# Moving gate transfers to GpSimd's queue and adding 11 places for raw weights in the feed-forward phases of a two-block transformer kernel

## The chip, the cores and the metric
The kernel runs on one core of a Trainium2 chip. The metric is the device time of one execution in microseconds (us). TensorE (PE) multiplies matrices, VectorE (DVE) and ScalarE (ACT) work elementwise, GpSimd (POOL) does almost nothing here, and SyncE (SP) only issues DMA transfers. Each engine takes its own instructions in a fixed order, and an instruction that waits holds up all that stand behind it on the same engine. This goes for the issuing of transfers as well.

## The reference
256 tokens of width 1024 in float32 pass through two blocks.

The first block has a mixer (latent attention with rotary positions, and a pooling branch), an attention over a memory of 256 rows, a mixture of 32 experts (two chosen for each token), and a norm.

The second block has two layers. What matters here is one layer, cut to this:

```python
mod = silu(c) @ ada_w[l] + ada_b[l]                 # 9 vectors of 1024
sh1, sc1, g1, sh2, sc2, g2, sh3, sc3, g3 = split(mod, 9)
n1 = rms_norm(h, norm_g[l, 0]) * (1 + sc1) + sh1
h = h + 0.5 * g1 * swiglu(n1, wg[l, 0], wu[l, 0], wd[l, 0])
n2 = rms_norm(h, norm_g[l, 1]) * (1 + sc2) + sh2
h = h + g2 * token_mixing(n2, ...)                  # two attentions, gates, an output product
n3 = rms_norm(h, norm_g[l, 2]) * (1 + sc3) + sh3
h = h + 0.5 * g3 * swiglu(n3, wg[l, 1], wu[l, 1], wd[l, 1])
```

`swiglu(x, wg, wu, wd)` is `(silu(x @ wg) * (x @ wu)) @ wd` with an inner width of 2816. So there are four feed-forward phases, and six gate vectors g that scale columns of a result.

## The kernel before, in words
**Weights come as a stream.** Every weight is used once, in pieces of 128 partitions by 1024 float32 columns (512 KB). A recording pass of the kernel notes the order of use; then the class `Stream` puts out, in that order, the load of a piece (on SP's queue, `w`), and for a piece of kind S its split into two parts of lower precision whose sum is the weight: `whi`, a rounded copy made by ACT in two halves (L205), and `wlo`, the rest `w - whi`, made by DVE in two halves (L212). PE needs three products for each pair of operands (L432 to L434: `whi` by the activations' high part, `wlo` by the high part, `whi` by the low part).

**Places.** A raw piece takes one of `N_RAW` = 4 places from its load until its `wlo` is made; `whi` and `wlo` have 8 places each (`N_HI`), held until PE has used the piece. `pump` issues what has a place: splits run up to 8 pieces ahead of PE, and loads at most 4 pieces ahead of the splits. A load therefore waits, on SP, for the DVE instruction that frees the place it will overwrite.

**Modulation pieces.** Pieces of kind A hold rows of the transposed `ada_w`. DVE multiplies each with silu(c) and sums along the row (`ajunk`, L623, two instructions of 512 columns and two short reads of the accumulator); eight pieces make one vector, a column tile `acolt`. `plan` lays 144 such pieces between the others: 16 early ones, and then 36, 16, 28, 28, 12 and 8 in the six phases of the second block (feed-forward, mixing, feed-forward, for each layer). They use raw places too.

**Gates.** A finished gate vector (`ada_finish`, L636 and L637) has to lie along the rows: its 1024 values are written from the column tile to DRAM (`gate`), and read back broadcast to all partitions (`growt`). Both transfers are issued by SP, so they stand between loads of weights, and the second waits for the first to land. The result is read by `res_gate` (L1509, tile `rg`) at the end of the phase that the gate belongs to.

**A feed-forward phase** (`ffn`) runs over 11 blocks of 256 inner columns. For block i, PE makes the two products of the gate and up weights (4 pieces, tile `ps`, 12 matmuls for each piece and both tiles of 128 tokens), ACT applies silu (`si`, L1543) and DVE multiplies (`pr`, L1545). While that happens PE does the down products of block i-1 (2 pieces, accumulated in `facc`), and between those of the first and the second tile of tokens it transposes `pr` (L438, `ps<-cst,pr`), which ACT and DVE split again (`hTh`, `hTl`). So PE waits for `pr`, and `pr` stands on DVE behind the splits and sums of pieces that are needed some 7 pieces later.

Every phase has a memory pool of its own, laid over the memory of the phase before; a tile of the new phase waits only for the last users of the tiles that lay there.

Of the kernel before, what the change touches and what calls it, by code (L numbers as in the profile page):

```python
# [18 lines left out]
P = 128  # L19
# [17 lines left out]
N_RAW = 4  # L37
N_HI = 8
# [7 lines left out]
# ---------------------------------------------------------------------------  # L46
# constants that depend on shapes alone
# ---------------------------------------------------------------------------
def _constants():
# [4 lines left out]
    # moe: [t', t] = 1 where t' < t  # L54
# [7 lines left out]
    # block 1 attention: chunk mask rows, added as two more rows of the contraction  # L62
# [6 lines left out]
    c["maskrows"] = np.stack([mq, mk], axis=1)  # [2, (q,k), S]  # L69
# [9 lines left out]
    )  # [p, g, t', tok]  # L79
# [3 lines left out]
    # block 2: axial angles, distances  # L83
# [4 lines left out]
    cs = np.stack([np.cos(ang), np.sin(ang)], axis=1).astype(np.float32)  # [S, 2, sec, 16]  # L88
# [8 lines left out]
# ---------------------------------------------------------------------------  # L97
# layout of the inputs
# ---------------------------------------------------------------------------
# [48 lines left out]
class Piece:  # L148
# [7 lines left out]
    def half(self, i):  # L156
        """Columns 512 i to 512 i + 511 of a piece of kind R."""
        if self.tag is None and len(self.place[0]) == 2:
            return self.place[0][i]
        raw = self.place[0][0] if self.tag is None else self.raw  # L160
        return raw[:, i * 512:(i + 1) * 512]


class Stream:
    """The weights in the order of their use: loads run ahead as far as slots are free. Kind S is split
    into two float32r parts ahead of its use; R is used as it is; A goes into a
    modulation vector."""

    def __init__(self, K, order):
        self.K = K  # L170
        self.rec = order is None
        self.order = [] if order is None else order
        self.pos = self.i_dma = self.i_hi = self.i_lo = self.clock = 0
        self.live = {"raw": 0, "hi": 0, "lo": 0}
        self.cap = {"raw": N_RAW, "hi": N_HI, "lo": N_HI}
        self.hold = math.inf  # from this piece on, no splits yet but those that must
        self.extra = []  # more places for pieces of kind R: its tiles, whether it can be used again
        self.deferred = []
        self.ada_done = {}

    def _load(self, p, tag):
# [7 lines left out]
        else:  # L189
            self.live[tag] += 1  # L190
            p.raw = K.wpool.tile([P, PIECE], F32, name="w", tag=tag, bufs=self.cap[tag])
            K.nc.sync.dma_start(p.raw[:, : p.n], K.piece_ap(p))

    @staticmethod
    def _halves(p):
        """In two, so that short steps of other chains get in between sooner."""
        return [slice(c, min(c + 512, p.n)) for c in range(0, p.n, 512)]
# [18 lines left out]
    def pump(self, upto=-1, raw=N_RAW):  # L216
        """Puts out the steps that can run by now, and those of the pieces up to a position anyhow."""
# [4 lines left out]
        while moved:  # L222
# [28 lines left out]
            while self.i_dma < len(order):  # L251
                p = order[self.i_dma]
                tags = ["raw", "hi", "lo"] if p.kind == "R" and self.i_lo >= self.i_dma else ["raw"]
                tag = next((x for x in tags if live[x] < cap[x]), None)
# [5 lines left out]

    def hold_after(self, n):
        """Holds back the splits after those of the next n pieces of kind S."""
# [46 lines left out]
    # modulation vectors: a piece for each 128 rows  # L309
# [28 lines left out]
def plan(order):  # L338
    """Places the pieces of the modulation weights among the others."""
# [11 lines left out]
    at = []  # (position, piece)  # L351
# [7 lines left out]
    # of the others, so many in each phase of the second block: the vector engine has more else to do in some  # L359
# [27 lines left out]
class Kernel:  # L387
# [28 lines left out]
    def load(self, dst, src):  # L416
        """Behind what is traced so far on its queue's engine, so not ahead of weights that are due before."""
# [22 lines left out]
    def rsqrt(self, y, v, t, scale, n=1):  # L440
        """y = scale * v ** -0.5 (all [P, n]; t is scratch): a first guess (within 3.4%) from the bits; then
        y <- ((v y^2)^2 + c1 v y^2 + c0) y, the minimax step within that range, which takes b v^-0.5 to
        (b^5 / k) v^-0.5 within 2.6e-5; then Newton's y <- (v y^2 - 3 g^2) y, from g v^-0.5 to -2 g^3 v^-0.5."""
# [20 lines left out]
    def warm(self, n, after=None, tag="mm"):  # L464
        """Products whose results nobody reads, so that the array's clock is not gated down while it has to wait."""
# [14 lines left out]
    def ss(self, dst, src, scale=1.0):  # L480
        """dst [P, 1] = sum of the squares of scale * src (up to 512 columns)."""
# [6 lines left out]
    def rstd(self, st, width, two=True):  # L488
        """(sum of squares / width + eps) ** -0.5 from the sums in st[:, 0:2]."""
# [8 lines left out]
    def split_T(self, hi, lo, src, gain=None):  # L498
        """hi/lo float32r of src * gain, gain per partition."""
# [8 lines left out]
    def transpose_split(self, hi, lo, src, kts, t, k0=0):  # L508
        """hi/lo[:, k0 + k, t's tokens] = src[:, k's columns] ^ T."""
# [29 lines left out]
    def dense(self, name, hi, lo, kt, width, src, evac, cb=512, tag="acc", outer=None, mid=None, pre=None, post=None):  # L539
        """A generator: for each block of columns, out[t] = x[t] @ w, then evac(t, b, out). Groups of  # L540
        outer blocks take all of one tile of tokens before the other; else the tiles take turns at each
        piece. mid follows the first group's first tile; pre(t, b) each evac; post(0)
        precedes the last tile's evac. Yields True between groups."""
# [66 lines left out]
    def c_silu(self):  # L610
        """silu(c) along the rows."""
# [3 lines left out]
    def ada_piece(self, l, m, i, raw):  # L615
        """128 outputs of a vector, by columns, from the transposed weights."""
# [9 lines left out]
    def ada_finish(self, l, m):  # L626
# [5 lines left out]
        elif m % 3 == 2:  # L632
            # along the rows, by way of DRAM
            d = self.dram.tile([D], F32, name="gate", tag="gate", bufs=2)
            col, r = r, self.ct([P, D], name="growt", tag="grow", bufs=3)
            nc.sync.dma_start(d.rearrange("(k p) -> p k", p=P), col)  # L636
            nc.sync.dma_start(r, d.unsqueeze(0).to_broadcast([P, D]))  # L637
        self.S.ada_done[(l, m)] = r

# [4 lines left out]
    def gain_row_pe(self, name, tile):  # L644
        """The same without a transfer for each partition; tile() gives places of 512 columns."""
# [15 lines left out]
    # =======================================================================  # L661
# [34 lines left out]
    def mixer(self, nrm):  # L696
# [3 lines left out]
        with self.phase("mix1") as pool:  # L700
# [14 lines left out]
            cs = self.ct([P, 2, 2, 16], name="cs")  # [p, (cos, sin), t, 16]  # L715
            rs = nrm.rs

            def tables():
                """rope tables of the positions"""
# [58 lines left out]
            def rope(x, t, heads, o1, o2):  # L778
                """x: [P, heads, 32] view, in place."""
# [39 lines left out]
            # pooling: d^T = u^T band, y^T = w^T d^T  # L819
# [9 lines left out]
            # gates and the pooling branch run between the steps of the attention  # L829
# [83 lines left out]
            def values(hp, p0, p1):  # L913
# [13 lines left out]
                # transposed, the two heads in their halves of the columns of the array  # L927
# [43 lines left out]
    def cross(self, nrm, pool):  # L971
# [26 lines left out]
        def to_T(dst, src, t, b):  # L998
            """dst[:, 4b.., t] = src ^ T, src [P, 512]."""
# [74 lines left out]
        # what the experts' phase starts with  # L1074
# [16 lines left out]
        # the output product, one tile of tokens after the other; the first two heads' half runs early  # L1091
# [56 lines left out]
    def moe(self, nrm, pool):  # L1148
# [16 lines left out]
        # the weights also use memory that other things need before or later  # L1165
# [1018 lines left out]
```

## Time and profile before

| | us |
|---|---|
| median of 3 runs | 1723.43 (1722.06 to 1725.42) |
| span of the profiled execution, first to last instruction | 1710.4 |
| median less that span | 13.0 |
| PE busy in the span | 1600.0 (94%) |
| DVE busy | 1139.6 (67%) |
| ACT busy | 817.2 (48%) |
| POOL busy | 0.2 |
| granted TensorE clock, mean over the span | 0.982 |

The page gives the span of the profiled execution and no device time of its own beside it; the 13.0 us are what the runs' median has more than that span, start and end of the program included. A busy share is an average over stages: the experts' stage (about 310 to 520 us) reads 512 KB pieces at 408 GB/s and is limited by that, and the four feed-forward phases, in which PE is busy 90 to 99%, are looked at one by one below.

### The profile page before, as it was taken

The numbers are of one execution on the slowest core, as the hardware profiler recorded it, in microseconds if no ns is written. First come the engines' busy times: TensorE is split into PE (matmuls) and PEld (weight loads), VectorE is DVE, ScalarE is ACT, GpSimd is POOL, SyncE is SP. The second block draws the span as 40 slices with busy tenths as digits, with TensorE's granted clock in tenths as the row PEclk, the third lists the DMA queues.
The fourth block names the chain that finished last, engine by engine and source line by source line (L and its number), as shares of the span: only waits on it lengthen the run. The fifth ranks groups of instructions, "written<-read, shape, count | busy, mean of one in ns | idle before, by whom it ended". The sixth has DMA issues, their size and how long they took to land.

```text
span 1710.4 us, 22657 instructions
## 1 busy us (share of the span) xinstructions
PE 1600.0 (94%) x7704; PEld 1197.0 (70%) x7704; DVE 1139.6 (67%) x2633; ACT 817.2 (48%) x1752; POOL 0.2 (0%) x4
## 2 busy tenths in 40 slices
PE   8999999788879989889999899999998999999998
PEld 7878887333115767667778787877876877878886
DVE  7878756111008878687889777778775788886664
ACT  5655642111006434366765444455443768474442
POOL 0000000000000000000000000000000000000000
PEclk9999999989999999999999999999999999999999
DMA  7667759799996898755576887858787744756663
GB/s 247 206 216 280 231 181 360 273 409 408 408 408 222 302 262 289 248 197 196 167 239 199 254 283 256 273 183 301 257 267 184 222 166 160 244 185 212 223 211 89
DMA packets 128645, 424.10 MB, mean 248 GB/s; under 512 B 21098, under 2 KB 23434, under 8 KB 128524
## 3 DMA queue, kind: packets, MB, share of 16 engines
q1 hardware_dynamic: 122160, 414.00, 70.5%
q10 hardware_dynamic: 6364, 8.60, 1.7%
q8 instruction: 62, 1.02, 0.2%
q14 instruction: 59, 0.48, 0.1%
HBM read 421.47 MB, written 1.07 MB: 247 GB/s over the span
## 4 chain that ended last, share of the span: by engine, by line
PE 33%; DMA 29%; DVE 11%; ACT 3%; issue 3%; SPq 0%; DVEq 0%; ACTq 0%
DMA w<-in_w_dram 19%; DMA w<-in_wm_dram 6%; DVE wlo L212 5%; PE d L432 4%; PE d L434 4%; PE d L433 4%; PE ps L433 3%; PE ps L434 3%; PE ps L432 3%; DVE ajunk L623 3%; PE ps L438 2%; DMA gate<-acolt 2%; PE facc L432 2%; PE facc L433 2%; PE facc L434 2%
## 5 line engine op out<-in xcount | busy, mean ns | idle before, releaser
L205 ACT ACTIVATE whi<-w 128x512 fp32r<-128x512 f32 (+1 forms) x888 | 513.6, 622 | 460.3 <-DMA w<-in_w_dram 314.3
L212 DVE TENSOR_TENSOR wlo<-w,whi 128x512 fp32r<-128x512 f32 (+1 forms) x888 | 574.3, 682 | 159.9 <-ACT whi L205 156.3
L432 PE MATMUL ps<-whi,xh 128*128 128x512 f32 x704 | 278.8, 396 | 0.8 <-ACT xh L2080 0.5
L433 PE MATMUL ps<-wlo,xh 128*128 128x512 f32 x704 | 275.3, 391 | 0.8 <-DVE wlo L212 0.7
L434 PE MATMUL ps<-whi,xl 128*128 128x512 f32 x704 | 275.1, 391 | 0.0
L432 PE MATMUL d<-whi,xh 128*128 128x512 f32 (+3 forms) x528 | 206.4, 391 | 0.2 <-ACT xh L2080 0.2
L433 PE MATMUL d<-wlo,xh 128*128 128x512 f32 (+3 forms) x528 | 203.5, 385 | 1.1 <-DVE stat L457 1.1
L434 PE MATMUL d<-whi,xl 128*128 128x512 f32 (+3 forms) x528 | 203.2, 385 | 1.0 <-DVE xl L503 1.0
L623 DVE CUSTOM_DVE_ANT_0 ajunk<-w,c_row,cols 128x512 bf16<-128x512 f32 x144 | 107.5, 746 | 95.5 <-DMA w<-in_w_dram 95.5
L433 PEld LDWEIGHTS ps<-wlo,xh 128*128 128x128 f32 x704 | 132.5, 188 | 28.2 <-DVE wlo L212 2.0
L432 PEld LDWEIGHTS ps<-whi,xh 128*128 128x128 f32 x704 | 132.4, 188 | 28.0 <-ACT xh L2080 1.2
L434 PEld LDWEIGHTS ps<-whi,xl 128*128 128x128 f32 x704 | 132.3, 188 | 28.0 <-DVE xl L2081 0.4
L432 PE MATMUL facc<-whi,hTh 128*128 128x512 f32 x352 | 144.9, 412 | 4.4 <-ACT hTh L502 4.4
L434 PE MATMUL facc<-whi,hTl 128*128 128x512 f32 x352 | 140.7, 400 | 1.1 <-DVE hTl L503 1.0
L433 PE MATMUL facc<-wlo,hTh 128*128 128x512 f32 x352 | 140.9, 400 | 0.0
L432 PEld LDWEIGHTS d<-whi,xh 128*128 128x128 f32 x528 | 100.2, 190 | 21.2 <-issue 3.6
L434 PEld LDWEIGHTS d<-whi,xl 128*128 128x128 f32 x528 | 100.3, 190 | 20.1 <-DVE xl L503 1.7
L433 PEld LDWEIGHTS d<-wlo,xh 128*128 128x128 f32 x528 | 100.4, 190 | 18.4 <-DVE wlo L212 1.7
L623 DVE CUSTOM_DVE_ANT_0 ajunk<-w,c_row,apart 128x512 bf16<-128x512 f32 x144 | 107.7, 748 | 3.1
L1399 PE MATMUL ps<-w,xg 128*32 128x512 f32 x472 | 86.3, 623 | 14.3 <-DMA w<-in_wm_dram 7.9
L432 PEld LDWEIGHTS facc<-whi,hTh 128*128 128x128 f32 x352 | 68.3, 194 | 19.4 <-ACT hTh L502 6.6
L434 PEld LDWEIGHTS facc<-whi,hTl 128*128 128x128 f32 x352 | 68.0, 193 | 17.3 <-DVE hTl L503 2.6
(405 smaller groups left out, 1855.2 us busy)
## 6 DMA issues: line engine op xcount, KB each, us to landing
w<-in_w_dram SPq DMA_DIRECT2D x578, 512.0 KB, 4.5
w<-in_wm_dram SPq DMA_DIRECT2D x163, 512.0 KB, 9.3
adaacc<-in_wm_dram SPq DMA_DIRECT2D x16, 512.0 KB, 10.2
xf<-in_wm_dram SPq DMA_DIRECT2D x16, 256.0 KB, 9.6
growt<-gate SPq DMA_DIRECT2D x6, 512.0 KB, 5.7
w<-in_w_dram SPq DMA_DIRECT2D x6, 384.0 KB, 3.7
growt<-in_rows_dram ACTq DMA_DIRECT2D x4, 512.0 KB, 6.0
bg<-in_rows_dram ACTq DMA_DIRECT2D x8, 256.0 KB, 4.7
```

What stands on the lines that cost most here:

```text
L205: K.nc.scalar.activation(p.hi[:, sl], p.raw[:, sl], AF.Copy)
L212: K.nc.vector.tensor_sub(p.lo[:, sl], p.raw[:, sl], p.hi[:, sl].bitcast(F32))
L432: mm(out, lhsT=xh, rhs=wh, start=start, stop=False)
L433: mm(out, lhsT=xh, rhs=wl, start=False, stop=False)
L434: mm(out, lhsT=xl, rhs=wh, start=False, stop=stop)
L438: self.nc.tensor.transpose(out, in_, self.ident[:k, :k])
L623: self.nc.vector.tensor_tensor_reduce(out=junk, in0=raw[:, sl], in1=self.c_row[:, sl], scale=1.0, scalar=acc, op0=ALU.mult, op1=ALU.add, a ...
L1399: T.matmul(gu[e * CAP:(e + 1) * CAP, :], lhsT=xg[j // 2][:, k, c:c + CAP], rhs=p.half(e % 2), start=(k == 0), stop=(k == KD - 1), tile_pos ...
```

## The change
The six pairs of gate transfers are issued on GpSimd's queue. In each feed-forward phase the phase's own pool holds 11 more places for raw pieces (`N_MORE`); until the last piece of that phase has been loaded, a load takes one of these if it can, else one of the four old ones. Pieces of the phases between (mixing) use the four old places as before. At the phase's start `more_places` pumps at once. The other edits take comments and docstrings out (lines of the new file stand up to 14 lower).

```diff
+N_MORE = 11
@@ class Stream
-        self.live = {"raw": 0, "hi": 0, "lo": 0}
-        self.cap = {"raw": N_RAW, "hi": N_HI, "lo": N_HI}
+        self.live = {"raw": 0, "hi": 0, "lo": 0, "more": 0}
+        self.cap = {"raw": N_RAW, "hi": N_HI, "lo": N_HI, "more": N_MORE}
+        self.more = None
+        self.more_end = -1
@@ _load
-            p.raw = K.wpool.tile([P, PIECE], F32, name="w", tag=tag, bufs=self.cap[tag])
+            pool = self.more if tag == "more" else K.wpool
+            p.raw = pool.tile([P, PIECE], F32, name="w", tag=tag, bufs=self.cap[tag])
@@ pump
                 tags = ["raw", "hi", "lo"] if p.kind == "R" and self.i_lo >= self.i_dma else ["raw"]
+                if self.i_dma <= self.more_end:
+                    tags = ["more", "raw"]
@@
+    def more_places(self, pool, last):
+        if not self.rec:
+            self.more = pool
+            self.more_end = next(i for i, p in enumerate(self.order) if p.key == last)
+            self.pump()
@@ ada_finish
-            nc.sync.dma_start(d.rearrange("(k p) -> p k", p=P), col)
-            nc.sync.dma_start(r, d.unsqueeze(0).to_broadcast([P, D]))
+            nc.gpsimd.dma_start(d.rearrange("(k p) -> p k", p=P), col)
+            nc.gpsimd.dma_start(r, d.unsqueeze(0).to_broadcast([P, D]))
@@ ffn
+            S_.more_places(pool, ("dn2", l, w, NFB - 1, 1))
```

SP's order before, around the first gate (first feed-forward phase). `w_5311`, `w_5313`, `w_5324` and so on are raw pieces; names in brackets are the semaphores that the issue waits for (DMAHW0 to 7 are those of transfers, taken in turn):

```order
L192 DMA w_5278<-in_w_dram 128x1024 [waits DMAHW1_49,DVE_49]
L636 DMA gate_5280<-acolt_4934 128x8x1
L192 DMA w_5311<-in_w_dram 128x1024 [waits DMAHW2_49,DVE_49]
L192 DMA w_5313<-in_w_dram 128x1024 [waits DMAHW3_49,DVE_49]
L637 DMA growt_5281<-gate_5280 128x1024 [waits DMAHW6_49]
L192 DMA w_5324<-in_w_dram 128x1024 [waits DMAHW4_49,DVE_49]
L192 DMA w_5376<-in_w_dram 128x1024 [waits DMAHW5_49,DVE_49]
L192 DMA w_5378<-in_w_dram 128x1024 [waits DMAHW7_49,DVE_49]
```

POOL's order with the change, from the first gate on:

```order
L649 DMA gate_5206<-acolt_4875 128x8x1 [waits DVE_49]
L650 DMA growt_5207<-gate_5206 128x1024 [waits DMAHW3_49,DMAHW7_49,DMASW0_49,PE_49]
L649 DMA gate_6208<-acolt_5875 128x8x1 [waits DVE_49]
L650 DMA growt_6209<-gate_6208 128x1024 [waits DMAHW4_49,DMAHW6_49,DMASW2_49,PE_49]
L649 DMA gate_8781<-acolt_8017 128x8x1 [waits DVE_49]
L650 DMA growt_8782<-gate_8781 128x1024 [waits DMAHW2_49,DMAHW5_49,DMASW4_49,Activation_49]
```

The pairs have left SP's order for POOL's, where nothing else stands; a wait of `growt` for `gate` now holds up POOL alone.

SP's order before, at the start of the first feed-forward phase (`c_row` is silu(c)'s row, which the sums need):

```order
L192 DMA w_4457<-in_w_dram 128x1024 [waits DMAHW2_49,DMAHW6_49,DVE_49,Activation_49]
L192 DMA w_4464<-in_w_dram 128x1024 [waits DMAHW3_49,DMAHW7_49,DVE_49,Activation_49]
L608 DMA c_row_4605<-in_c_row_dram 128x1024 [waits DMAHW4_49,PE_49]
L192 DMA w_4638<-in_w_dram 128x1024 [waits DMAHW0_49,DMAHW5_49,DVE_49,Activation_49]
L192 DMA w_4640<-in_w_dram 128x1024 [waits DMAHW1_49,DVE_49]
L192 DMA w_4642<-in_w_dram 128x1024 [waits DMAHW2_49,DVE_49]
L192 DMA w_4644<-in_w_dram 128x1024 [waits DMAHW3_49,DVE_49]
```

The same place with the change:

```order
L196 DMA w_4615<-in_w_dram 128x1024 [waits DMAHW2_49,DVE_49,Activation_49]
L196 DMA w_4457<-in_w_dram 128x1024 [waits DMAHW3_49,DMAHW6_49,DVE_49,Activation_49]
L196 DMA w_4464<-in_w_dram 128x1024 [waits DMAHW4_49,DMAHW7_49,DVE_49,Activation_49]
L621 DMA c_row_4605<-in_c_row_dram 128x1024 [waits DMAHW5_49,PE_49]
L196 DMA w_4617<-in_w_dram 128x1024 [waits PE_49]
L196 DMA w_4619<-in_w_dram 128x1024 [waits PE_49]
L196 DMA w_4621<-in_w_dram 128x1024 [waits DMAHW0_49]
L196 DMA w_4623<-in_w_dram 128x1024 [waits DMAHW1_49]
L196 DMA w_4625<-in_w_dram 128x1024 [waits DMAHW2_49]
L196 DMA w_4627<-in_w_dram 128x1024 [waits DMAHW3_49]
L196 DMA w_4629<-in_w_dram 128x1024 [waits DMAHW4_49]
L196 DMA w_4631<-in_w_dram 128x1024 [waits DMAHW5_49]
```

From `w_4621` on the loads wait for earlier transfers only, not for DVE; before, each of these rows waited for a split on DVE. `w_4617` and `w_4619` wait for the last products of the experts' phase, whose memory they take over.

DVE's order before, between two steps of the first feed-forward phase; the pieces are those of the first fence:

```order
L503 TENSOR_TENSOR hTl_5188<-ps_5184,hTh_5187 128x256
L623 ISA ajunk_5370,apart_5369<-w_5311,c_row_4605,cols_69 128x512
L623 ISA apart_5369 128x1
L623 ISA ajunk_5370,acolt_5268<-w_5311,c_row_4605,apart_5369 128x512
L623 ISA acolt_5268 128x1
L212 TENSOR_TENSOR wlo_5392<-w_5313,whi_5373 128x512 x2
L623 ISA ajunk_5396,apart_5395<-w_5324,c_row_4605,cols_69 128x512
L623 ISA apart_5395 128x1
L623 ISA ajunk_5396,acolt_5268<-w_5324,c_row_4605,apart_5395 128x512
L623 ISA acolt_5268 128x1
L212 TENSOR_TENSOR wlo_5421<-w_5376,whi_5415 128x512 x2
L212 TENSOR_TENSOR wlo_5438<-w_5378,whi_5418 128x512 x2
```

The next row there is `pr_5292`. With the change the rows ahead of a `pr` at this point of the phase are of the same kinds:

```order
L636 ISA ajunk_5482,apart_5481<-w_5204,c_row_4605,cols_69 128x512
L636 ISA apart_5481 128x1
L636 ISA ajunk_5482,acolt_5197<-w_5204,c_row_4605,apart_5481 128x512
L636 ISA acolt_5197 128x1
L216 TENSOR_TENSOR wlo_5367<-w_5151,whi_5344 128x512 x2
L636 ISA ajunk_5489,apart_5488<-w_5242,c_row_4605,cols_69 128x512
L636 ISA apart_5488 128x1
L216 TENSOR_TENSOR wlo_5401<-w_5155,whi_5364 128x512 x2
L1559 TENSOR_TENSOR pr_5386<-ps_5293,si_5384 128x256
```

Splits and sums still stand ahead of `pr`; what moved is the place of their loads on SP, which stand up to 11 pieces further ahead.

## Rows read from the trace of the kernel before

**Rows 1.** Windows by stage, core 0: four feed-forward phases and one mixing phase.
```profile
core 0: us, PE busy (x) PEld busy (x) DVE busy (x) ACT busy (x) POOL busy (x), PEclk, DMA share, GB/s
534.90:749.60 214.70, 193.94 (x849) 155.87 (x850) 164.40 (x352) 99.63 (x203) 0.00 (x0) 0.97 0.79 260
749.60:930.20 180.60, 175.09 (x909) 138.97 (x909) 148.18 (x361) 116.98 (x280) 0.00 (x0) 1.00 0.60 198
930.20:1131.50 201.30, 191.70 (x851) 155.00 (x850) 149.67 (x323) 98.83 (x199) 0.00 (x0) 0.98 0.76 254
1131.50:1334.20 202.70, 192.03 (x856) 155.68 (x856) 149.31 (x325) 98.16 (x200) 0.00 (x0) 0.98 0.76 247
...
1513.80:1702.00 188.20, 186.69 (x845) 152.66 (x843) 118.05 (x232) 90.11 (x181) 0.00 (x0) 1.00 0.62 196
```

**Rows 2.** PE's waits, 534.9 to 749.6: us in total, times, longest.
```profile
PE ps L438 <- DVE pr L1545: 17.7, 7, 6.1
PE facc L432 <- ACT hTh L502: 1.3, 1, 1.3
```

**Rows 3.** PE's waits, 930.2 to 1131.5.
```profile
PE ps L438 <- DVE pr L1545: 7.7, 4, 4.9
PE facc L432 <- ACT hTh L502: 1.6, 1, 1.6
```

**Rows 4.** PE's waits, 1131.5 to 1334.2, and then 1513.8 to 1702.
```profile
PE ps L438 <- DVE pr L1545: 10.0, 3, 6.6
...
PE facc L432 <- ACT hTh L502: 1.5, 1, 1.5
```

**Rows 5.** All waits of the span, of ACT, DVE and SP.
```profile
ACT whi L205 <- DMA w<-in_w_dram: 314.3, 176, 9.4
...
DVE ajunk L623 <- DMA w<-in_w_dram: 95.5, 60, 5.3
...
SPq L637 <- DMA gate<-acolt: 49.2, 6, 9.3
```

**Rows 6.** Timeline of SP, 590 to 625: start, length, instruction.
```profile
596.01 0.42 SPq L636 DMA_DIRECT2D gate<-acolt  x1
...
608.03 0.33 SPq L637 DMA_DIRECT2D growt<-gate  x1
```

**Rows 7.** Timeline of DVE, 606 to 619.3; in brackets idle before and releaser.
```profile
608.67 0.75 DVE L623 CUSTOM_DVE_ANT_0 ajunk<-w,c_row,cols 128x512 bf16<-128x512 f32 x1 [1.60 <-DMA w<-in_w_dram]
...
618.83 0.42 DVE L1545 TENSOR_TENSOR pr<-ps,si 128x256 f32<-128x256 f32 x1
```

**Rows 8.** Timeline of PE, at the first and the last of the long waits.
```profile
619.30 0.69 PE L438 MATMUL ps<-cst,pr 128*128 128x128 f32 x2 [5.68 <-DVE pr L1545]
...
1305.18 0.69 PE L438 MATMUL ps<-cst,pr 128*128 128x128 f32 x2 [6.58 <-DVE pr L1545]
```

**Rows 9.** Windows: two stretches at half clock, and one of the first block.
```profile
616.70:623.60 6.90, 4.30 (x11) 3.46 (x12) 6.29 (x14) 3.24 (x8) 0.00 (x0) 0.51 0.87 306
978.60:982.00 3.40, 3.40 (x10) 2.72 (x11) 3.06 (x8) 2.07 (x4) 0.00 (x0) 0.50 0.89 341
100.00:200.00 100.00, 99.93 (x484) 81.85 (x484) 87.18 (x186) 57.62 (x116) 0.00 (x0) 1.00 0.72 253
```

**Rows 10.** Windows ahead of the first gate's write, and while it runs.
```profile
580.00:595.00 15.00, 15.00 (x69) 12.40 (x68) 12.66 (x29) 6.51 (x13) 0.00 (x0) 1.00 0.86 320
599.00:608.00 9.00, 9.00 (x42) 7.43 (x41) 3.26 (x6) 2.31 (x6) 0.00 (x0) 1.00 1.09 99
```

**Rows 11.** DMA issues of the whole span: count, KB each, median us to landing.
```profile
growt<-gate SPq DMA_DIRECT2D x6, 512.0 KB, 5.7
...
gate<-acolt SPq DMA_DIRECT2D x6, 4.0 KB, 10.0
```

**Rows 12.** The last gate: timeline of SP, and of DVE.
```profile
1672.92 0.33 SPq L637 DMA_DIRECT2D growt<-gate  x1
...
1690.16 0.69 DVE L1509 SCALAR_TENSOR_TENSOR rg<-facc,growt 128x512 f32<-128x512 f32 x1 [1.29 <-PE facc L434]
```

## The prediction
> **What bounds the kernel now.** I began with windows by stage [rows 1]. The four feed-forward phases do the same products (845 to 856 matmuls), yet take 214.7, 201.3, 202.7 and 188.2 us. The last is nearly full: PE is busy 186.7 of 188.2 us at full clock. In the other three PE is busy 192 to 194 us, more than in the last, at a mean clock of 0.97 or 0.98, and idle the rest. So they lose 26.5, 13.1 and 14.5 us against the last phase, 54.1 us in all; the reader is to see that the loss is largest where the plan puts 36 modulation pieces, middling where it puts 28, and absent where it puts 8.
>
> Next, PE's waits in each phase [rows 2 to 4]. Nearly all idle time ends with DVE's `pr`: 17.7, 7.7 and 10.0 us, with 1.3 and 1.6 us for `hTh`; 38.3 us together. `pr` is short, so the question is what DVE did before. In the waits of the span [rows 5], ACT's copies waited 314.3 us for weights' transfers and DVE's sums 95.5 us. On DVE the `pr` that PE wanted at 613.6 us stood behind sums and splits of pieces needed only some 7 pieces later; the piece at 608.67 had just landed, and `pr` started at 618.83 [rows 7], 5.68 us after PE had nothing left [rows 8]. A late load thus stops PE at once, although its weights are not due.
>
> Why was it late? SP issued the gate's write at 596.01 and its reading back at 608.03 [rows 6], since the second waits for the first: 49.2 us of waiting in the six pairs [rows 5], and the loads behind stood still. The long waits of PE come 17 to 19 us after a gate: 5.68, 6.1 (with 1.3 for `hTh`), 4.9, 1.6 and 6.58 us, 26 us together (first and last of five in [rows 8], the others the longest of [rows 2, 3]). After each, the clock is at its lower level, 1.2 GHz, three times for 6.8 to 6.9 us and twice for 3.4 us (one of each in [rows 9]): 27.3 us at half speed, 13.7 us lost. The other 12.1 us of waits (38.3 less 26.2) follow no gate: there four raw places were too few. 38.3 + 13.7 = 52.0 of the 54.1 us; the rest are gaps too short for a row.
>
> **The change part by part.** *Gates to POOL's queue.* SP loses twelve issues, and the stops between the pairs (49.2 us of waits) go. The instructions themselves are 0.42 and 0.33 us on SP [rows 6], six of each, and SP is not what PE waits for once loads run ahead, so I count the stops alone. On POOL they wait in front of nobody. The transfers stay: the write of 1024 single values took 10.0 us to land and the reading back 5.7 us [rows 11]. What the write does to loads beside it is in [rows 10]: with it under way the DMA engines were busy over their full share (1.09) and moved 99 GB/s, against 320 GB/s at a share of 0.86 shortly before. So for about 10 us loads crawl, whichever queue issued the gate, and only loads that have landed already can cover that.
>
> The Trainium skill has a rule for this, DMA: Bandwidth & Descriptors, section "Issuing engines are not separate DMA queues": another issuing engine saves the sequencer's time alone, the same 16 DMA engines run the transfer. The trace agrees in that the share was full during the write (1.09); by the rule alone, without the added places, the queue's move would leave the crawl.
>
> *Eleven places.* Loads may stand 15 instead of 4 pieces ahead of the splits. A phase with 36 modulation pieces uses 66 + 36 = 102 pieces, at 190 us one in 1.86 us, so a full set lasts 28 us (30 us at 94 pieces). A load lands in under 10 us, leaving some 18 us, more than the 12 us between a gate's two issues [rows 6] and the 10 us of crawl. The refill needs 102 x 0.524 MB in 190 us, 281 GB/s; 320 GB/s was already moved with four places [rows 10]. The new loads wait at the phase's start for products of the phase before (the order shows two such rows), but these come on top of four loads already issued, so I cost that at nothing; if that cover is gone it costs what rival 4 counts.
>
> With loads early, DVE's sums stop waiting, and the splits wait for PE to free their 8 places, as they did in the last phase, whose order is the same. What is late next? DVE, in the first phase: 164.4 us of work for 188.2 us, 87% [rows 1]; in the two others 149 to 150 us, 80%. In a stretch of the first block DVE was busy 87.2% and PE 99.93% [rows 9], so that share need not hold PE up. But `pr` keeps its place behind splits, so some short waits may stay: between 0 and the 12.1 us that follow no gate. I take 5 us, nearer to the end that the stretch at 87.2% shows.
>
> *POOL's way of issuing.* The trace has no transfer of POOL's, so no price for one. A gate needs to be there at its phase's end. The tightest is the last: read back issued at 1672.92, landed about 1678.6, used at 1690.16 [rows 12], 11.5 us to spare; its last sum stands five `pr` earlier in DVE's order now, and two `pr` are a block of 188.2 / 11 = 17.1 us, so some 40 us are added. The price lies between nothing and, were a POOL transfer to take all of 15.7 us [rows 11] more than SP's, still nothing; I take 0.
>
> A page of the skill speaks against the move: SBUF — State Buffer, section "SBUF: two separate sides", holds that GpSimd can't write the descriptors of its transfers while DVE runs certain two-port instructions. No run here shows it yet; by it the gate would come later, and the 50 us to spare would have to be used up before the sum changes.
>
> *Sum.* 54.1 - 5 = 49 us off the span: 1710.4 - 49 = 1661.4 us. The median of the runs is 13.0 us above the profiled span (1723.43 - 1710.4), which I carry over: 1674.4 us, 2.8% faster. The mixing phases (180.6 us, PE busy 175.1 [rows 1]), the first block and the experts hold no gate transfers and no new places, and stay. If the ends of the residue are taken, 0 and 12.1, the time is 1669 to 1681; reading errors of the phases' borders and small gains in the mixing phases, whose first pieces are loaded earlier, widen this to 1664 to 1685.
>
> **Rivals.**
> 1. *The crawl still reaches PE.* The places are not full when a gate is written (they are shared with modulation pieces, and transfers take turns on eight semaphores), so of the 26.2 + 13.7 = 39.9 us behind gates half stays. For it: the share of 1.09 [rows 10]. Against: 18 us of cover for 10 us. Time: 1674 + 20 = 1694.
> 2. *DVE's order becomes the bound.* If the feed-forward order cannot run DVE above the 82% of the mixing phase (148.18 of 180.60), the first phase takes 164.4 / 0.82 = 200 us instead of about 191, the others fit. For it: `pr` keeps its place. Against: 87.2% in [rows 9]. Time: 1674 + 10 = 1684.
> 3. *GpSimd holds DVE up: slower.* While POOL prepares the 1024 single values, DVE's instructions with two SBUF operands (every split, every sum) cannot run. At the nearest row, 10.0 us for each write [rows 11], six writes cost 60 us: 1674 + 60 = 1734. It decides from 49 / 6 = 8.2 us a gate. For it: DVE is busy 80 to 87% where the gates are made, so nothing hides a stop. Against: preparing 4 KB would have to stop another engine entirely, for as long as the whole write takes to land. The skill's page cited above has the stop the other way round.
> 4. *The change does not do what it says:* the new places come free so late (memory of the phase before) that the first loads are held, each of the four phase starts losing about what a gate cost, 26.2 / 5 = 5 us plus 3 us at half clock: 4 x 8 = 32 back, 1706. Against: the second added load waits for the last product of the phase before, which ends before the new phase's first.
>
> **How the numbers follow.** Forecast 72%, rival 1 10%, rival 2 9%, rival 3 3%, rival 4 4%, and 2% for no difference. A measurement of this kernel can tell 0.2%, 3.4 us, from no change. Faster than that are the forecast and rivals 1, 2 and 4: 95%; slower 3%; within 2%. The likeliest case's own range is 1664 to 1685; to leave out no more than 2 in 10, I go up to rivals 1 and 2: 1662 to 1695.
>
> **What would show it.** Right: the three long phases at 189 to 192 us each, no half clock in them; DVE's waits for transfers in `ajunk` nearly gone from the feed-forward phases, ACT's copies waiting for PE instead; loads landing 15 to 30 us ahead of their split; gate transfers on a queue of POOL's. Wrong: waits of 4 us or more for `pr` 15 to 20 us after a gate (rival 1); steady waits of 1 us for `pr` in each block of the first phase with DVE near 90% (rival 2); splits longer than before or DVE gaps beside POOL's issues (rival 3); PE idle at phase starts (rival 4).

## The result, and the profile after

| | before | after |
|---|---|---|
| median of the runs, us | 1722.74 (1721.93 to 1725.42, 4 runs) | 1662.44 (1661.25 to 1664.02, 4 runs) |
| ratio | 1 | 0.9664, interval 0.9637 to 0.9692 |
| span of the profiled execution, us | 1710.4 | 1660.7 |

The change made the kernel 3.4% faster; 1674.4 us (2.8%) were forecast. The time lies 0.4 us inside the stated range of 1662 to 1695, and below the 1664 to 1685 of the likeliest case. The span was forecast at 1661.4 and came out at 1660.7 us. One execution of the kernel with the queue's move alone, the first one profiled, ran at a mean granted clock of 0.651 and took 2235.29 us; its ratio leaves it out.

The windows by stage of the changed kernel, columns as in [rows 1]: the four feed-forward phases, and the two mixing phases as second and fifth row.

```profile
534.70:722.20 187.50, 187.46 (x849) 153.36 (x849) 162.17 (x352) 99.18 (x201) 3.05 (x4) 1.00 0.82 292
722.20:901.90 179.70, 175.75 (x908) 140.27 (x909) 147.89 (x361) 119.74 (x283) 0.00 (x0) 0.99 0.64 213
901.90:1092.50 190.60, 190.52 (x865) 155.97 (x865) 150.31 (x326) 96.98 (x195) 2.91 (x4) 1.00 0.75 261
1092.50:1284.50 192.00, 188.38 (x841) 151.99 (x840) 147.64 (x322) 99.02 (x200) 1.46 (x2) 0.99 0.74 256
1284.50:1465.40 180.90, 177.14 (x909) 140.70 (x909) 142.97 (x342) 119.47 (x283) 0.00 (x0) 0.99 0.62 206
1465.40:1652.20 186.80, 186.75 (x845) 152.75 (x843) 117.90 (x232) 89.76 (x180) 1.46 (x2) 1.00 0.54 177
```

Against [rows 1] the four feed-forward phases are 27.2, 10.7, 10.7 and 1.4 us shorter, 50.0 together; the mixing phases stay. PE is idle for 0.04, 0.08, 3.62 and 0.05 us in them; of the 3.62 us, 2.38 are one wait for `pr` and the rest four short waits in the first 9 us of that phase. The first phase, the worst before, has become as short as the last, with DVE busy for 162.17 of 187.50 us (86%).

Next the waits: of PE in the phase from 1092.5 to 1284.5 (total us, times, longest), the only one with a wait for `pr`.

```profile
PE ps L451 <- DVE pr L1559: 2.4, 1, 2.4
```

And the waits of the whole span that answer to [rows 5].

```profile
ACT whi L209 <- PE ps L447: 131.6, 108, 1.6
ACT whi L209 <- DMA w<-in_w_dram: 81.2, 66, 5.2
...
POOL growt L650 <- DMA gate<-acolt: 46.9, 4, 13.9
DVE ajunk L636 <- DMA w<-in_w_dram: 29.5, 20, 7.6
```

ACT's waits for transfers fell from 314.3 to 81.2 us, and its copies now wait for PE to free a place. DVE's sums wait 29.5 instead of 95.5 us. The waits of `growt` have not become shorter: 46.9 us for `gate` in four of the six pairs (49.2 us in all six before), and 22.4 us in the other two, which the profile puts down to the products whose place `growt` takes over. But they are on POOL, where nothing stands behind them.

The gate transfers by themselves: issues of the whole span, answering to [rows 11] (KB each, median us to landing), then POOL's timeline at the first and the last gate.

```profile
growt<-gate POOLq DMA_DIRECT2D x6, 512.0 KB, 7.8
...
gate<-acolt POOLq DMA_DIRECT2D x6, 4.0 KB, 11.6
```

```profile
580.18 1.03 POOL L649 DMA_DIRECT2D gate<-acolt  x1 [579.73 <-DVE acolt L636]
591.68 0.56 POOL L650 DMA_DIRECT2D growt<-gate  x1 [10.47 <-PE ps L447]
...
1576.07 0.90 POOL L649 DMA_DIRECT2D gate<-acolt  x1 [348.06 <-DVE acolt L636]
1587.87 0.56 POOL L650 DMA_DIRECT2D growt<-gate  x1 [10.90 <-DMA gate<-acolt]
```

A pair costs POOL some 1.5 us of its own, more than the 0.75 us on SP [rows 6]. That the write's median landing is 11.6 us here and 10.0 us in [rows 11] shows no price of POOL: the trace of before tells only two of the six landings (9.1 and 10.9 us), and the two that the places alone tell, on SP's queue, are 10.7 and 12.2 us. The last pair is issued 85 us earlier than in [rows 12], 35 more than the kernel as a whole, and its reader comes 52.6 us after the second issue, some 45 after the landing (DVE's timeline):

```profile
1640.46 0.69 DVE L1522 SCALAR_TENSOR_TENSOR rg<-facc,growt 128x512 f32<-128x512 f32 x1 [1.28 <-PE facc L447]
```

Has the slow stretch gone? Three windows: the first gate's write, the fifth, and a stretch of 3.5 us of PE after the fifth.

```profile
580.20:591.10 10.90, 10.90 (x51) 8.99 (x50) 10.70 (x24) 5.95 (x12) 1.02 (x1) 1.00 0.95 182
...
1213.60:1227.20 13.60, 13.60 (x64) 11.18 (x63) 4.93 (x12) 6.96 (x14) 0.00 (x0) 1.00 1.12 191
1238.90:1242.40 3.50, 3.43 (x12) 2.79 (x13) 1.28 (x5) 0.38 (x1) 0.00 (x0) 0.68 0.82 298
```

No: beside these two writes the DMA engines are about as full as in [rows 10] (0.95 and 1.12) and move 182 and 191 GB/s, well under the 292 and 256 of their phases as a whole. Beside the other four writes they move still less, 96 to 144 GB/s, at a share of only 0.45 to 0.82; so a full share is not what marks the slow stretch, as [rows 10], read from one gate, would have it. What changed is that PE works through what follows: it stays busy after the first write, where [rows 8, 9] showed 5.68 us of idle time and 6.9 us at half clock. One gate is still felt, the fifth, whose write is the longest (14.5 us): loads issued beside it took 14.9 to 16.0 us to land, those beside the other four of the first five gates at most 12.2 us, as far as the trace tells them. DVE's timeline, then PE's:

```profile
1228.48 0.75 DVE L636 CUSTOM_DVE_ANT_0 ajunk<-w,c_row,cols 128x512 bf16<-128x512 f32 x1 [7.61 <-DMA w<-in_w_dram]
```

```profile
1238.97 0.44 PE L451 MATMUL ps<-cst,pr 128*128 128x128 f32 x2 [2.38 <-DVE pr L1559]
```

A sum waits 7.61 us for its piece, `pr` comes late, PE is idle for 2.38 us, and from 1.2 us later on its matmuls take 0.63 instead of 0.39 us for 3.4 us, at a granted clock of 0.5. That is the chain of [rows 7, 8] in small.

### The profile page after: what moved, and what is told of

Read it like the earlier page. It is cut to its first block, busy times and chain, and to the rows that moved or that the text cites. A ratio compares the mean times of both kernels' runs of the same rounds, so it can differ in the third digit from the quotient of the medians.

```text
span 1660.7 us, 22566 instructions
## 1 busy us (share of the span) xinstructions
PE 1590.9 (96%) x7704; PEld 1191.5 (72%) x7704; DVE 1136.4 (68%) x2633; ACT 818.6 (49%) x1752; POOL 9.1 (1%) x16
## 3 DMA queue, kind: packets, MB, share of 16 engines
q0 software_dynamic: 1056, 3.17, 0.5%
## 4 chain that ended last, share of the span: by engine, by line
PE 62%; DMA 11%; DVE 5%; ACT 2%; issue 1%; DVEq 0%; ACTq 0%; SPq 0%
PE ps L445 9%; PE ps L447 9%; PE ps L446 9%; DMA w<-in_wm_dram 5%; PE facc L445 5%; PE facc L447 5%; PE facc L446 5%; PE d L445 4%; PE d L446 4%; PE d L447 4%; DMA w<-in_w_dram 4%; PE ps L451 3%; DVE wlo L216 2%; PE y L1448 1%; DMA adaacc<-in_wm_dram 1%; PE ps L1412 1%
## 5 line engine op out<-in xcount | busy, mean ns | idle before, releaser
L445 PE MATMUL facc<-whi,hTh 128*128 128x512 f32 x352 | 141.5, 402 | 0.1
L636 DVE CUSTOM_DVE_ANT_0 ajunk<-w,c_row,cols 128x512 bf16<-128x512 f32 x144 | 107.5, 746 | 29.8 <-DMA w<-in_w_dram 29.5
```

Of the source, the lines that this page charges most:

```text
L445: mm(out, lhsT=xh, rhs=wh, start=start, stop=False)
L636: self.nc.vector.tensor_tensor_reduce(out=junk, in0=raw[:, sl], in1=self.c_row[:, sl], scale=1.0, scalar=acc, op0=ALU.mult, op1=ALU.add, a ...
```

## The experiments

Theory A, the prediction's: a gate's write slows the loads beside it for 10 to 14 us, whichever queue issues it, and the places bring loads far enough ahead to cover that; the queue's move adds little. Rival Q: SP's stops behind the gate are what cost, and the queue is the cure. Rival P: the places would have helped without any gate, since four were too few. All ratios are against the kernel before, run on the same chip. "Lead" is worked out from a trace: for each piece the time from the issue of its load to the start of the first instruction that reads it, as the median of the splits or the sums of a feed-forward phase; ranges are those of the first three phases. A wait for the load's landing is part of it.

**The kernel before, again.**

> The kernel before once more, to see each run's span beside its time. Theory A: about 2.2 us lie around the span (as in the changed kernel, 1662.86 - 1660.7), so the runs of 1722 to 1725 us have spans of about 1720 to 1723, and the profiled span of 1710.4 was a faster execution; the long phases of the timed runs then lose some 10 us more than the 54 us read from that profile. Theory B: about 13 us lie around the span in this kernel and the spans are about 1710.

Measured: 1720.33 us (1711.77 to 1729.27, 10 runs), ratio 0.9988 (0.9963 to 1.0014). The profiled one was the shortest of the ten: 1711.77 us for a span of 1710.0. Over the 49 executions of this kernel in the study the time is 1.72 to 1.85 us more than the span, and the spans go from 1710.0 to 1730.5 us. The ten shortest have a mean granted clock of 0.982, the four longest of 0.976, though single ones stray (one of the four has 0.981). So the 13.0 us are not something around the span: 1.8 us are, and some 11 us are lost inside the span by the usual execution and not by the profiled one. An estimate from the spans and clocks of the 49: half speed cost 36.9 us on average and 30.8 us in the profiled execution, so 6 of the 10 us by which the average span (1720.5) exceeds the profiled one. Which waits did it was not seen, as no long execution was profiled.

**The places alone.**

```diff
-            nc.gpsimd.dma_start(d.rearrange("(k p) -> p k", p=P), col)
-            nc.gpsimd.dma_start(r, d.unsqueeze(0).to_broadcast([P, D]))
+            nc.sync.dma_start(d.rearrange("(k p) -> p k", p=P), col)
+            nc.sync.dma_start(r, d.unsqueeze(0).to_broadcast([P, D]))
```

> The 11 places alone; the gates' transfers stay on SP's queue. Theory A (what counts is how long ahead of their use the loads land; splits' loads are now issued 25 to 38 us ahead of use, sums' loads 12 to 15 us): a stop of 12 us on SP is covered for the splits and not quite for the sums, so most of the gain stays: about 1672 us, some DVE waits for ajunk's loads after gates. Rival (SP's stops are the cost): about 1700 us, PE waits of 4 to 6 us after the gates remain.

Measured: 1660.56 us (1657.80 to 1663.56), ratio 0.9645 (0.9623 to 0.9667), the whole gain, and 11 us less than theory A said. SP's timeline at the fifth gate, and the waits of DVE's sums in the span (the longest 3.5 us):

```profile
1221.75 3.28 SPq L196 DMA_DIRECT2D w<-in_w_dram  x2
1225.08 0.43 SPq L649 DMA_DIRECT2D gate<-acolt  x1
1234.07 0.33 SPq L650 DMA_DIRECT2D growt<-gate  x1
1234.45 1.45 SPq L196 DMA_DIRECT2D w<-in_w_dram  x2
```

```profile
DVE ajunk L636 <- DMA w<-in_w_dram: 23.7, 17, 3.5
```

SP does stop for 9 us, and no row shows PE waiting for `pr`. Rival Q falls for the kernel with 11 added places.

**The queue alone**, run twice; the rows are of the second.

```diff
-N_MORE = 11  (and all that uses it)
```

> The gates on GpSimd's queue alone; four raw places. Theory A (the write of 1024 single values slows every load beside it, whichever queue issued it, and with four places nothing covers that): 1705 to 1715 us, PE waits of 3 to 6 us after the gates remain. Rival (SP's stops are the cost): about 40 us less than before, 1683 us.

> The queue's move alone once more, for its trace (its first profile fell on a chip at a lower clock throughout). Theory A: 1705 to 1715 us again; in the trace SP issues loads beside the gate's write, which land 10 us and more later, and PE's waits of 3 to 6 us after the gates are still there. Rival: they are gone and waits elsewhere took their place.

Measured: 1712.25 us, ratio 0.9945 (0.9923 to 0.9967), and 1715.60 us (10 runs), ratio 0.9975 (0.9953 to 0.9997). PE's timeline behind the first gate, and DVE's wait:

```profile
624.10 0.69 PE L438 MATMUL ps<-cst,pr 128*128 128x128 f32 x2 [6.94 <-DVE pr L1545]
```

```profile
DVE ajunk L623 <- DMA w<-in_w_dram: 107.1, 62, 8.2
```

The stops are gone from SP, which now issues two to four loads beside each write; but behind four of the first five gates loads take 9 to 12 us to land, and PE waits longer behind the first gate than in [rows 8]. The move is worth 0.25 to 0.55% by itself, as theory A said; the rival's 1683 us are refuted. The rule of the Trainium skill that the prediction cited (DMA: Bandwidth & Descriptors, "Issuing engines are not separate DMA queues") is borne out: beside the first five writes 107 to 178 GB/s were moved, 109 to 144 before, so another issuer left the slow stretch slow.

**A short write, four places.** The kernel before, with the gate's values written as 128 runs of 8 instead of 1024 single values; they land in another order.

```diff
-            nc.sync.dma_start(d.rearrange("(k p) -> p k", p=P), col)
+            nc.sync.dma_start(d.rearrange("(p k) -> p k", p=P), col)
```

> The kernel before with each gate written to DRAM as 128 runs of 8 values instead of 1024 single values (the values land in another order, so columns are scaled with other columns' gates). The write should land in 2 to 4 us instead of 10. Theory A (crawl and stop together make the gates' cost of about 40 us, and both last as long as the write): the stop shrinks to about 4 us and the crawl goes, 1685 to 1695 us. Rival (the cost is the two issues' order on SP itself): under 10 us gained.

Measured: 1686.34 us (1682.39 to 1690.22), ratio 0.9789 (0.9769 to 0.9809). The write's landing, SP's timeline at the first gate, and PE's waits for `pr` from 530 to 1330:

```profile
gate<-acolt SPq DMA_DIRECT2D x6, 4.0 KB, 5.1
```

```profile
601.14 0.42 SPq L636 DMA_DIRECT2D gate<-acolt  x1
602.30 2.13 SPq L192 DMA_DIRECT2D w<-in_w_dram  x2
605.77 0.33 SPq L637 DMA_DIRECT2D growt<-gate  x1
```

```profile
PE ps L438 <- DVE pr L1545: 16.6, 12, 3.4
```

The write lands in 5.1 instead of 10.0 us (two landings each; 2 to 4 us were expected), PE's longest wait is 3.4 instead of 6.6 us, and 36 us of the 60 are gained with no added place. By the profiled spans, which set one of the shortest executions of before against the longest of the four here, it is 22 us of 50. So some half of what the places gain is what the write cost; 12 short waits are left. The short write shortens both the slow stretch and SP's stop; as the queue's move, which takes away the stop alone, gained 4 to 10 us, most of the 36 us is left to the slow stretch.

**The short write with the change.**

> The changed kernel with each gate written as 128 runs of 8 values (the values land in another order, so columns are scaled with other columns' gates). Theory A: the slow stretch goes, and with it the one PE wait of 2.4 us behind the fifth gate and its half clock: 1657 to 1661 us. Rival (that wait is no matter of the write): 1662 us.

Measured: 1662.28 us (1660.36 to 1666.69), ratio 0.9670 (0.9650 to 0.9690). The write's landing, and the waits of DVE's sums:

```profile
gate<-acolt POOLq DMA_DIRECT2D x6, 4.0 KB, 4.7
```

```profile
DVE ajunk L636 <- DMA w<-in_w_dram: 14.8, 15, 2.6
```

No wait for `pr` is left in the feed-forward phases, the one behind the fifth gate included, so that wait was a matter of the write. But theory A's 1657 to 1661 us missed: the profiled span is 2.0 us shorter than with the long write, and the runs don't tell 1662.28 from 1662.44. Against the short write with four places (1686.34) the added places still gain 24 us (20 by the two ratios, each against the same chip): rival P is right to that extent, and 36 + 24 is the whole gain of 60.

**Fewer places, 4 and then 7.**

```diff
-N_MORE = 11
+N_MORE = 4      (second kernel: 7)
```

> The changed kernel with 4 more places instead of 11 (8 raw places in all). Theory A (loads have to land some 12 to 15 us ahead of use to ride out a gate's write): 8 places last about 8 x 1.9 = 15 us less the landing, too little for a write of 11 us beside which loads crawl, so some PE waits of 2 to 4 us after gates, 1668 to 1676 us. Rival (any places beyond four do): 1662 us.

> The changed kernel with 7 added places instead of 11 (with 4 it took 1689.2 us, with 11 1662.4). Theory A (the lead grows with the places, 11.7 to 14.4 us of lead for splits at 4 and 25 to 38 us at 11, so about 18 to 22 us here, above the 11 to 14.6 us that a gate's write takes): most of the gain, 1664 to 1674, with one or two waits of PE for pr left. Rival (all eleven are needed): on the straight line between, 1689.2 - 3/7 x 26.8 = 1678, or above.

Measured: 1689.19 us (1687.80 to 1690.42), ratio 0.9817 (0.9801 to 0.9834), and 1685.51 us (1681.18 to 1687.91), ratio 0.9759 (0.9721 to 0.9797). Both are above what theory A said; the rival of the second expectation, 1678 us or above, holds. PE's waits for `pr` in the stretch of the first three feed-forward phases, with 4 and with 7:

```profile
PE ps L451 <- DVE pr L1559: 19.4, 7, 6.0
```

```profile
PE ps L451 <- DVE pr L1559: 16.8, 5, 6.0
```

With 7, the longest wait of a sum (DVE's timeline), 14.5 us after the second gate's write was issued:

```profile
687.62 0.75 DVE L636 CUSTOM_DVE_ANT_0 ajunk<-w,c_row,cols 128x512 bf16<-128x512 f32 x1 [8.01 <-DMA w<-in_w_dram]
```

| places added | lead of splits, us | lead of sums, us | waits for `pr`, us | time, us | ratio |
|---|---|---|---|---|---|
| 0 | 5 | 5 | 35.4 | 1722.7 | 1 |
| 4 | 12 to 14 | 6 to 7 | 19.4 | 1689.2 | 0.9817 |
| 7 | 17 to 21 | 6 to 10 | 16.8 | 1685.5 | 0.9759 |
| 11 | 25 to 29 | 12 to 16 | 2.4 | 1662.4 | 0.9664 |

With 7 places the splits' lead is already longer than a gate's write, but that of the sums is not, and the waits stay. A sum is put into DVE's order soon after its load, well before its vector is due, and has about half the lead of a split. It is the first to be late behind the second and the fifth gate, and `pr` stands behind it all the same; behind the third gate the longest of DVE's waits ended with a split (3.62 us). So the lead to look at first is the sums', and seven places were not enough; 8 to 10 were not run.

**Each gate written twice, side by side.**

```diff
+            d2 = self.dram.tile([D], F32, name="gatex", tag="gatex", bufs=2)
+            nc.gpsimd.dma_start(d2.rearrange("(k p) -> p k", p=P), col)
             nc.gpsimd.dma_start(d.rearrange("(k p) -> p k", p=P), col)
```

> The changed kernel with each gate written to DRAM twice, one write behind the other on GpSimd's queue (the first to a tile that nobody reads). Theory A: the slow stretch grows from 11 to some 20 us; splits (25 to 38 us ahead) ride it out, the sums (12 to 15 us ahead) do not, so DVE waits for ajunk's loads after most gates and PE loses 3 to 6 us at four or five of them: 1675 to 1690 us. Rival (the places cover it all): within 5 us of 1662.

Measured: 1665.42 us (1664.25 to 1668.84), ratio 0.9678 (0.9662 to 0.9694). The rival's number held and theory A's missed, but by the trace the edit did not do what it was for. Windows over the first two pairs of writes:

```profile
583.00:595.00 12.00, 12.00 (x55) 9.90 (x54) 11.77 (x27) 6.50 (x14) 1.91 (x2) 1.00 0.78 153
674.80:688.00 13.20, 13.20 (x62) 10.86 (x61) 10.87 (x25) 6.42 (x14) 1.77 (x2) 1.00 0.45 128
```

The two writes ran beside each other and landed in 11 to 12 us (medians), the time that one takes, so the stretch was no longer than before. It settles nothing on the cover; hence the next pair.

**Each gate written twice, one after the other**, on GpSimd's queue and then, with the places kept, on SP's.

```diff
             nc.gpsimd.dma_start(d.rearrange("(k p) -> p k", p=P), col)
+            nc.gpsimd.dma_start(d.rearrange("(k p) -> p k", p=P), col)
```

> The changed kernel, with each gate written twice one after the other (the second write waits for the first to land), so that the slow stretch of loads lasts some 23 us for each gate instead of 11 to 14.6 (landings of the gate's write in the changed kernel). Theory A (the places cover the stretch because loads land 25 to 38 us ahead of their split and 12 to 15 us ahead of their sum): 23 us is more than the sums' lead, so sums hold DVE up again behind the five gates of the first three phases, PE waits 2 to 6 us for pr behind each and loses 3.4 us at half clock: 1672 to 1690 us. Rival (the lead is far more than any such stretch needs, as the two writes side by side at 1665 suggested): within 3 us of 1662.

> The same doubled writes one after the other, with all gate transfers on SP's queue and the 11 places kept. Theory A (the crawl itself is what costs, whichever queue issues the gate): the same as its twin on GpSimd's queue, within 5 us, 1672 to 1690 us. Rival (on SP the loads also stand still behind two waits of some 11 us, which the places no longer hide): 10 us or more above its twin, 1685 to 1705.

Measured: 1673.75 us (1669.55 to 1682.72), ratio 0.9704 (0.9654 to 0.9755) on GpSimd's queue, and 1685.26 us (1681.28 to 1689.23), ratio 0.9773 (0.9736 to 0.9811) on SP's. POOL's timeline at the fifth gate, then PE's waits for `pr` in the second and third feed-forward phases, on GpSimd's queue and on SP's:

```profile
1224.17 0.89 POOL L649 DMA_DIRECT2D gate<-acolt  x1 [145.99 <-DVE acolt L636]
1237.63 0.88 POOL L650 DMA_DIRECT2D gate<-acolt  x1 [12.57 <-DMA gate<-acolt]
1250.80 0.56 POOL L651 DMA_DIRECT2D growt<-gate  x1 [12.28 <-DMA gate<-acolt]
```

```profile
PE ps L451 <- DVE pr L1560: 7.0, 3, 4.0
```

```profile
PE ps L451 <- DVE pr L1560: 14.9, 2, 7.7
```

Waits are back behind two of the five gates, the third and the fifth, and 11 us are lost (7 by the two ratios, whose intervals overlap). That is in theory A's range, at its low end, but theory A had waits behind all five. From the first write's issue to the reading back it takes 24.3, 24.6, 26.8, 20.2 and 26.6 us at the five gates: all outlast the sums' lead, and only the two longest come through. So the lead against the length of the stretch tells which load is late first, and not by itself when PE is stopped. The twin on SP's queue was to be within 5 us and is 11.5 us longer, with 8 us more of PE's waits, as the rival said. Here theory A is too simple; it looks as if, where the lead is used up, loads that crawl are better than loads that aren't issued. The two intervals just overlap, so this is a strong hint and no more.

## Why the prediction came out as it did

- **The loss of 54.1 us and its cause**: right. The three phases gave back 48.6 us (the last one 1.4 more). The prediction put 39.9 us behind the gates; the short write, which leaves the places as they were, gained 36.
- **Gates to POOL's queue**, counted as the stops alone: by itself 0.25 to 0.55%; with the places nothing that the runs tell from zero (1660.56 without it, 1662.44 with it). The gain forecast for the two parts together comes with the places.
- **Eleven places, "18 us" of cover**: right in the outcome, wrong in the reason. The 28 us for a full set describe the splits (25 to 29); the sums have 12 to 16 us, hardly more than the 11 to 14.5 us of a gate's write. Nor does a load land in under 10 us beside a write: up to 16.0 us were seen. The cover was just enough, not ample, as 7 places and the doubled write showed. That it was enough is in part luck, since the sums' lead was not in the working.
- **A residue of 5 us**: the size was right, 3.6 us idle and some 1.7 us lost at half clock, but not its kind, so that it fits is luck. It was to be short waits from DVE's order; 4.1 us of it is one gate that is still felt, whose wait goes with the short write, and 1.2 us the start of the third phase.
- **POOL's way of issuing at 0**: held; some 45 us were to spare at the last gate. The page that spoke against the move (the Trainium skill, SBUF — State Buffer, "SBUF: two separate sides") would have had the writes held up by DVE: the first gate landed within 11 us with DVE busy for 10.70 of 10.90 us, and with four places the median landing was 10.7 us from POOL and 10.0 us from SP, so no run here shows it.
- **The 13.0 us carried over**: the step that failed, and nearly all of the 12 us by which the forecast was off. "The median of the runs is 13.0 us above the profiled span ..., which I carry over" took it for something outside the span. Outside are 1.8 us (2.2 after); the rest was time that before's usual execution loses inside the span and the profiled one did not, and it went with the change: the medians differ by 60.3 us, the profiled spans by 49.7. In which waits it was lost stays open. With 2.2 in place of 13.0 the same sum gives 1663.6. The range held the time by 0.4 us, by luck: its lower end was put at 1662 instead of 1664 with no term in the working for it.
- **Rival 1** holds for one gate of five, 4 of the 20 us that it gave. **Rival 2** is refuted by 86% of DVE beside a full PE. **Rival 3** too: `wlo` takes 684 ns on average, 682 before, and DVE is busy for 10.70 of 10.90 us beside the first gate's write. The section that the prediction named against this rival (the Trainium skill, SBUF — State Buffer, "SBUF: two separate sides") has the lock on the shared ports go to whichever of DVE and GpSimd starts first and block the other, so it did not speak against it; the run does. **Rival 4** has 1.2 us of waits at one phase's start behind it, not 8 us at each.

## What to carry to other kernels

A buffer's depth covers a disturbance least for the consumer with the shortest lead: work out, for each kind, the time from the issue of a load to its first use, and compare that with the longest stretch in which loads are slow, rather than taking the average over all pieces. Before adding buffers, look for the transfer that makes the stretch; here a write of 4 KB in single values was behind some half of what eleven places of 512 KB hid. And a median well above a profiled span is a reason to ask whether that execution was an easy one, since a change may take away what the trace doesn't show.

## What was not expected of the hardware

- Two writes of 1024 single values issued 0.9 us apart land in about the time of one (11.1 and 12.2 us against 11.6).
- A write of the same 4 KB as 128 runs of 8 values lands in 5.1 instead of 10.0 us on SP's queue and in 4.7 instead of 11.6 us on POOL's. On POOL's queue the number of packets is the same for both (1056 in the span, the readings back included), so there it is not more packets that make the single values slow.
- An issue of a gate's write takes 0.90 us on POOL and 0.42 us on SP, and programs that issue on POOL have 2.0 to 2.2 us outside their span where those that don't have 1.7 to 1.85.
